# Layer 0's output weights applied to a pair of blocks by seven products of quarters

## The chip, the core and the metric

The kernel runs on one core of one Trainium2 chip. The metric is the device time of one execution in microseconds. TensorE (PE) does the matmuls, with its weight loads shown as PEld; VectorE (DVE) and ScalarE (ACT) work on tiles; GpSimd (POOL) and SyncE (SP) mostly issue DMAs.

## What is computed

Two layers over 2048 tokens of 1024 channels, each with a gated residual; the change lies in the first, a chunked gMLP:

```python
u, v, gate = jnp.split(h @ w_in, 3, axis=-1)          # h: normalised, modulated x
u = jax.nn.gelu(u)
v = _layernorm(jax.nn.gelu(v), vn_g, vn_b)
s = jnp.einsum('gpq,bnqgc->bnpgc', w_s, vc) + b_s...  # vc: v in chunks of 128 tokens
y = u * s.reshape(bn, L, A_WIDTH)                     # A_WIDTH = 2048
return (y * jax.nn.silu(gate)) @ w_out                # w_out: 2048 x 1024
...
x = x + gate[:, None] * y
```

Layer 1 is a multi-scale pooling mixer of the same widths, followed by a last RMSNorm. All of it is in float32.

## The kernel before

Channels lie on partitions, tokens along the free axis. The 2048 tokens are four blocks of 512 (`TB`), worked on in pairs of 1024 (`W2`). Every float32 product is made of three matmuls over operands that are split into a high and a low part (`mm3`, lines 103 to 107): high by high, low by high, high by low. `put` (lines 109 to 112) makes the split: ACT casts to the high part (L110), DVE subtracts to get the low part (L111).

Layer 0 runs for each pair of blocks:

- `v_phase`: the v branch, for the pair.
- `b_phase0`: for each c of 8, two channel chunks of u and of the gate. Each is a `unit` of seven products of quarters (Strassen's scheme in Winograd's form: seven products in place of eight, with sums of quarters of the rows and of the weights ahead of the products and sums of products after them). `mix(c)` does the spatial product and DVE multiplies. The result for each chunk and block, a tile `s`, goes to `y_d` in DRAM by a DMA that POOL issues (L930).
- `c_phase` (called from `c_phase0`) for each of the two blocks apart, the output stage: 16 channel chunks of y, by 8 output chunks d, by three matmuls of 512 columns into eight PSUM banks `po`. Four such calls make the layer's output, 4 x 16 x 8 x 3 = 1536 matmuls. At the end of a call each bank is scaled by the gate and added to x, by DVE (L945) or by ACT and DVE in turn, and stored in `x1_d`.

Operands come through a `Stream`: an ordered list of jobs, each a load that SP issues and a split. `get(i)` sees to it that jobs up to i + `ahead` are split, and loads run up to `LEAD` jobs further. Loads land in `raw` tiles (6 in layer 0); y comes into tiles `s`. Split pairs have 9 places.

Work that nothing near needs is put in a queue, `side`, and `do_side(n)` runs n of its steps at fixed points: one after each product of a unit. In `b_phase0` of the first pair it holds the RMS statistics of the next two blocks (`fetched_rms`, squares summed in a tile `ra`, each over a freshly loaded tile `x`) and five groups of `ada_late` steps (a step loads an `x` tile of 512 columns and DVE multiplies and adds it into `ra`, L444; after eight of them TensorE sums over partitions, `pm`, L450). In the output stage it holds `sum_steps`, which makes the row quarters of the next pair: 60 DVE instructions in all. In the second `v_phase` it holds `sum_quarters`, which makes sums of quarters of a weight ahead of their use and keeps them in DRAM.

TensorE works in the order in which the instructions stand in its queue, as each engine does; a layer of the language below the kernel sets that order from the order of the code and the dependences.

Of the kernel before, what the change touches and what calls it, by code (L numbers as in the profile page):

```python
# [12 lines left out]
F32 = mybir.dt.float32  # L13
F32R = mybir.dt.float32r
AF = mybir.ActivationFunctionType
ALU = mybir.AluOpType

P = 128
D = 1024
L = 2048  # L20
# [43 lines left out]
def hybrid_kernel(ctx: ExitStack, tc: tile.TileContext, a: dict):  # L64
# [11 lines left out]
    x1_d = dram.tile([KD, P, L], F32, name="x1_d")  # L76
    x2_d = dram.tile([KD, P, W2], F32, name="x2_d")
    v_d = dram.tile([2, 8, P, 8, 2 * P], F32, name="v_d")
    y_d = dram.tile([NC, P, L], F32, name="y_d")
    y1_d = dram.tile([NC, P, L], F32, name="y1_d")  # L80
    bt_d = dram.tile([8, P, 2 * P], F32, name="bt_d")

# [8 lines left out]
    def work(tag, width=512):  # L91
        return wk.tile([P, WK[tag][0]], F32, name=tag, tag=tag, bufs=WK[tag][1])[:, 0:width]
# [22 lines left out]
    def do_side(n=1000):  # L115
        for _ in range(min(n, len(side))):
            side.popleft()()
# [4 lines left out]
    def st_load(dst, src):  # L122
        st.last = nc.sync.dma_start(dst, src).ins

    def load(dst, src):

        with tc.issue_after(st.last):
            nc.sync.dma_start(dst, src)
# [10 lines left out]
    def split(src):  # L139
        p = new_pair()  # L140
        put(p, src)
        return p
# [147 lines left out]
        return [two_units(unit_jobs(lambda kh, c=c: a["g_wu"][c, kh]), unit_jobs(lambda kh, c=c: a["g_wg"][c, kh]), False)  # L290
                for c in range(8)]

    def y0_job(c, b):
        box = []

        def load():
            box.append(work("s"))
            st_load(box[0], y_d[c, :, b * TB:(b + 1) * TB])

        return load, lambda: split(box[0])  # L300

    def c_jobs(y, w):

        jobs = []
        for c in range(0, NC, 2):
            h = [half_jobs(lambda c=c: w[c]) for c in (c, c + 1)]
            i = st.add(y(c), h[0][0], y(c + 1), h[1][0], h[0][1], h[1][1])
            jobs.append(((i[0], i[2]), (i[1], i[3]), (i[4], i[5])))
        return jobs

    def c0_jobs(b):
        return c_jobs(lambda c: y0_job(c, b), a["g_wo"])

    def y1_job(c, t0, n, pair):
        box = []
# [40 lines left out]
    for b in (0, 2):  # L356
        jv.append(v_jobs())
        jug.append(ug_jobs())
        jc0 += [c0_jobs(b), c0_jobs(b + 1)]

    def pg_jobs():
        return [two_units(unit_jobs_made(c, partial(wf, c)),
# [95 lines left out]
    def ada_late(i, *gs):  # L458
        return [f for g in gs for f in ada_steps(i, g, 4, lambda: work("x"), lambda: work("ra"))]
# [258 lines left out]
    def rhs_lhs(g):  # L718
        return jf[g]

    def sum_quarters(c, q):

        box = []

        def fetch():
            for kh in range(2):
                for o in (0, 512):
                    box.append(work(("x", "x", "ra", "th")[len(box)]))
                    nc.gpsimd.dma_start(box[-1], q(kh)[:, o:o + 512])

        def sums():
            b11, b12, b21, b22 = box
            tc.keep_in_program_order(nc.vector.tensor_sub(b11, b12, b11))
            nc.vector.tensor_sub(b12, b22, b12)
            nc.vector.tensor_sub(b22, b22, b11)
            nc.vector.tensor_sub(b21, b21, b22)
            for j in range(4):
                nc.gpsimd.dma_start(t_d[c, j // 2, :, (j % 2) * 512:(j % 2) * 512 + 512], box[j])

        return [fetch, sums]  # L740

# [124 lines left out]
    def spatial(pb, stats):  # L866
# [39 lines left out]

        return fetch, normalise, mix

    def b_phase0(bb, rows, stats):
        st.ahead = 4  # L910
        fetch, normalise, mix = spatial(bb, stats)
        fetch(0)
        normalise(0)
        for c in range(8):
            gu = [work("g") for _ in range(4)]
            u = unit(rows, jug[bb][c][0], gu, lambda j: nc.scalar.activation(gu[j], gu[j], AF.Gelu_apprx_tanh))
            for i, pn in enumerate(ORDER):
                u(pn)
                if i == 3:
                    ss = mix(c)  # L920
            for j in (0, 2, 3, 1):
                nc.vector.tensor_mul(ss[j], ss[j], gu[j])
            gt = [work("g") for _ in range(4)]

            def gate(j):
                cc, t0 = 2 * c + j % 2, bb * W2 + (j // 2) * TB
                s = ss[j]
                nc.scalar.activation(gt[j], gt[j], AF.Silu)
                nc.vector.tensor_mul(s, s, gt[j])
                nc.gpsimd.dma_start(y_d[cc, :, t0:t0 + TB], s)  # L930

            g = unit(rows, jug[bb][c][1], gt, gate)
            for i, pn in enumerate(ORDER):
                g(pn)
                if c < 7 and i == 0:
                    fetch(c + 1)
                if c < 7 and i == 3:
                    normalise(c + 1)
        do_side()

    def residual(d, x, po, gate, turns=True):
# [35 lines left out]
            residual(d, x, po[d][:, 0:n], gate)  # L977
            nc.gpsimd.dma_start(store[d, :, t0:t0 + n], x)

    def c_phase0(b):  # L980
        c_phase(jc0[b], b * TB, TB, a["xT"], mod[0], "s", x1_d)


    tsum = [sum_quarters(c, partial(wf, c)) for c in range(8)]


    side.extend(late[1] + bias_steps())
# [3 lines left out]
    for b in (2, 3):  # L991
        rms, steps = fetched_rms(src0(b), TB, "ra", "x", 5)
        rms0.append(rms)
        side.extend(steps)
    side.extend(ada_late(0, 16, 20) + ada_late(1, 0, 4, 8))
    b_phase0(0, rows, stats)
    rows = Rows(0, [src0(2), src0(3)], rms0)
    sums = rows.sum_steps(lambda: work("g"))
    side.extend(sums[:9])
    c_phase0(0)  # L1000
    side.extend(sums[9:])
    c_phase0(1)
    do_side()


# [9 lines left out]
    b_phase0(1, rows, stats)  # L1015
    rows = Rows(1, [src1(0), src1(1)], rms1)
    sums = rows.sum_steps(lambda: work("g"))
    side.extend(sums[:9])
    c_phase0(2)
    side.extend(sums[9:])  # L1020
    c_phase0(3)
    do_side()
    l0_stack.close()
    st.end = len(st.jobs)
# [229 lines left out]
```

## Time and profile before

| | us |
|---|---|
| median of 3 runs (lowest to highest) | 2464.91 (2464.88 to 2468.14) |
| the profiled execution | 2464.14 |
| its span | 2462.4 |
| PE busy | 2429.4 (99%) |
| DVE busy | 1844.7 (75%) |
| ACT busy | 1086.6 (44%) |
| mean moved by DMA | 170 GB/s (169 GB/s of HBM reads and writes) |

Shares are of the span. A matmul's entry lasts longer than the time until the next one starts, since they are pipelined; the time that one costs is the distance between starts. The same holds, to a smaller degree, for DVE instructions in a row.

### The profile page before, as it was taken

The numbers are of one execution on the slowest core, as the hardware profiler recorded it, in microseconds if no ns is written. First come the engines' busy times: TensorE is split into PE (matmuls) and PEld (weight loads), VectorE is DVE, ScalarE is ACT, GpSimd is POOL, SyncE is SP. The second block draws the span as 40 slices with busy tenths as digits, with TensorE's granted clock in tenths as the row PEclk, the third lists the DMA queues.
The fourth block names the chain that finished last, engine by engine and source line by source line (L and its number), as shares of the span: only waits on it lengthen the run. The fifth ranks groups of instructions, "written<-read, shape, count | busy, mean of one in ns | idle before, by whom it ended". The sixth has DMA issues, their size and how long they took to land.

```text
span 2462.4 us, 32915 instructions
## 1 busy us (share of the span) xinstructions
PE 2429.4 (99%) x11392; PEld 2045.7 (83%) x11392; DVE 1844.7 (75%) x3079; ACT 1086.6 (44%) x1862; POOL 259.3 (11%) x478
## 2 busy tenths in 40 slices
PE   8999999999999999999999999999999999999998
PEld 7768888888878888888888888888878888888998
DVE  6785788887854678877878548788876498988656
ACT  5844544443643445444436433333354333333533
POOL 2211100000000332000000001011000001100011
PEclk9999999999999999999999999999999999999999
DMA  9733434554664666343536644432457545445764
GB/s 351 266 122 112 149 123 135 157 170 133 220 219 163 226 222 209 115 135 111 172 121 219 234 146 149 141 106 99 141 184 238 179 139 178 139 144 166 226 194 145
DMA packets 170966, 418.43 MB, mean 170 GB/s; under 512 B 21408, under 2 KB 45984, under 8 KB 169776
## 3 DMA queue, kind: packets, MB, share of 16 engines
q1 hardware_dynamic: 138960, 314.01, 40.2%
q0 software_dynamic: 27808, 97.57, 10.8%
q10 hardware_dynamic: 4032, 4.75, 0.7%
q8 instruction: 90, 1.47, 0.2%
q14 instruction: 76, 0.62, 0.1%
HBM read 327.16 MB, written 89.10 MB: 169 GB/s over the span
## 4 chain that ended last, share of the span: by engine, by line
PE 76%; issue 14%; DVE 4%; DMA 4%; POOL 1%; ACT 1%; SPq 0%; POOLq 0%; DVEq 0%; ACTq 0%
PE pu L104 13%; PE pu L106 13%; PE pu L105 13%; PE po L106 8%; PE po L104 8%; PE po L105 8%; PE pa L104 2%; PE pa L105 2%; PE pa L106 2%; PE psp L896 2%; PE pv L105 1%; PE pv L104 1%; PE pv L106 1%; DMA raw<-in_pool_wpT 1%; DVE wlo L111 1%
## 5 line engine op out<-in xcount | busy, mean ns | idle before, releaser
L110 ACT CAST whi<-raw 128x512 fp32r<-128x512 f32 x816 | 492.3, 618 | 674.7 <-PE pu L105 265.8
L111 DVE TENSOR_TENSOR wlo<-raw,whi 128x512 fp32r<-128x512 f32 x816 | 548.5, 685 | 257.8 <-ACT whi L110 254.2
L104 PE MATMUL pu<-S,whi 128*128 128x512 f32 x1024 | 400.9, 392 | 0.0
L106 PE MATMUL pu<-S,wlo 128*128 128x512 f32 x1024 | 398.7, 389 | 0.0
L105 PE MATMUL pu<-S,whi 128*128 128x512 f32 x1024 | 398.5, 389 | 0.0
L104 PE MATMUL po<-whi 128*128 128x512 f32 (+1 forms) x768 | 299.9, 390 | 4.4 <-ACT whi L110 4.4
L106 PE MATMUL po<-whi,wlo 128*128 128x512 f32 (+1 forms) x768 | 299.8, 391 | 1.0 <-DVE wlo L111 1.0
L104 PE MATMUL pu<-A,whi 128*128 128x512 f32 x768 | 300.0, 391 | 0.0
L105 PE MATMUL po<-wlo,whi 128*128 128x512 f32 (+1 forms) x768 | 299.1, 390 | 0.0
L106 PE MATMUL pu<-A,wlo 128*128 128x512 f32 x768 | 299.0, 389 | 0.0
L105 PE MATMUL pu<-A,whi 128*128 128x512 f32 x768 | 298.8, 389 | 0.0
L106 PEld LDWEIGHTS pu<-S,wlo 128*128 128x128 f32 x1024 | 192.2, 188 | 40.4
L104 PEld LDWEIGHTS pu<-S,whi 128*128 128x128 f32 x1024 | 192.3, 188 | 39.2
L105 PEld LDWEIGHTS pu<-S,whi 128*128 128x128 f32 x1024 | 192.3, 188 | 39.0
L104 PEld LDWEIGHTS po<-whi 128*128 128x128 f32 x768 | 144.5, 188 | 36.1 <-ACT whi L110 6.1
L106 PEld LDWEIGHTS po<-whi,wlo 128*128 128x128 f32 x768 | 144.5, 188 | 33.1 <-DVE wlo L111 2.8
L105 PEld LDWEIGHTS po<-wlo,whi 128*128 128x128 f32 x768 | 144.4, 188 | 30.1
L106 PEld LDWEIGHTS pu<-A,wlo 128*128 128x128 f32 x768 | 144.1, 188 | 30.3
L105 PEld LDWEIGHTS pu<-A,whi 128*128 128x128 f32 x768 | 144.2, 188 | 29.6
L104 PEld LDWEIGHTS pu<-A,whi 128*128 128x128 f32 x768 | 144.2, 188 | 29.6
L104 PE MATMUL po<-big,whi 128*128 128x388 f32 (+1 forms) x384 | 123.2, 321 | 0.0
L105 PE MATMUL po<-big,whi 128*128 128x388 f32 (+1 forms) x384 | 122.8, 320 | 0.0
(232 smaller groups left out, 3935.6 us busy)
## 6 DMA issues: line engine op xcount, KB each, us to landing
raw<-in_g_wo SPq DMA_DIRECT2D x64, 512.0 KB, 4.2
raw<-in_p_wo SPq DMA_DIRECT2D x96, 256.0 KB, 3.2
v_d<-g POOLq DMA_DIRECT2D x64, 256.0 KB, 3.1
raw<-in_g_wu SPq DMA_DIRECT2D x32, 512.0 KB, 4.1
raw<-in_g_wg SPq DMA_DIRECT2D x32, 512.0 KB, 4.9
raw<-v_d SPq DMA_DIRECT2D x32, 512.0 KB, 4.6
y_d<-s POOLq DMA_DIRECT2D x64, 256.0 KB, 2.9
x<-in_ada_w SPq DMA_DIRECT2D x64, 256.0 KB, 3.1
```

Source lines behind the costliest of these rows:

```text
L104: nc.tensor.matmul(out, w[0], x[0], start=first and not onto, stop=False, skip_group_check=onto)
L105: nc.tensor.matmul(out, w[0], x[1], start=False, stop=False, skip_group_check=onto)
L106: nc.tensor.matmul(out, w[1], x[0], start=False, stop=last, skip_group_check=onto)
L110: nc.scalar.copy(pair[0], src)
L111: nc.vector.tensor_sub(pair[1], src, pair[0].bitcast(F32))
L896: nc.tensor.matmul(p[:, t * P:(t + 1) * P], vt[h][:, t * 2 * P + j * P:t * 2 * P + (j + 1) * P], bw[:, 0:P], start=True, stop=True)
```

## The change

The output stage of layer 0 now takes both blocks of a pair together and is itself done by seven products of quarters. The quarters of the operand are, for each k of 8, the two channel chunks of that k by the two blocks; the quarters of the weights are two chunks of 128 rows by two halves of 512 output channels. One of the seven products is 8 values of k by 4 output chunks by 3 matmuls, so that a pair takes 7 x 96 = 672 matmuls and the layer 1344.

- **Row sums.** After each c of `b_phase0`, `row_sums` makes four sums of the four `s` tiles on DVE and stores them through POOL. Of the four `s` tiles three are stored as they are, so that `y_d` gets seven tiles for each c in place of four.
- **Weight sums.** `sum_quarters` makes four sums for each k once, in the `side` queue of the first `b_phase0` (8 times 4 DVE instructions, 4 loads and 4 stores through POOL, spaced out by empty steps), and keeps them in `to_d`. Both pairs read them.
- **Pace.** In the gate's unit two side steps run after each product in place of one.
- **Output stage.** `c_pairs` replaces `c_phase` for layer 0. Each step loads two tiles of 128x512 (one of y, one of weights) into one `raw` tile, splits both, and runs 12 matmuls. After each product four DVE instructions add the banks to x (`onto`): 28 for a pair, where 16 DVE and 8 ACT instructions stood. x is loaded through POOL four tiles at a time. `LEAD` is 8 there.
- `sum_steps` runs evenly over the 56 steps of the pair's output stage.

```diff
-    y_d = dram.tile([NC, P, L], F32, name="y_d")
+    y_d = dram.tile([2, 8, 7, P, TB], F32, name="y_d")
+    to_d = dram.tile([8, 2, P, W2], F32, name="to_d")
...
+    CORDER = (1, 2, 6, 5, 7, 3, 4)
+
+    def co_jobs(y, w, t):
+
+        src = {1: lambda k: w(k, 0)[:, 0:512], 2: lambda k: w(k, 1)[:, 0:512], 3: lambda k: w(k, 1)[:, 512:W2],
+               5: lambda k: t[k, 0][:, 0:512], 7: lambda k: t[k, 0][:, 512:W2],
+               4: lambda k: t[k, 1][:, 0:512], 6: lambda k: t[k, 1][:, 512:W2]}
+
+        def two(k, pn):
+            box = []
+
+            def load():
+                box.append(raw_tile())
+                st_load(box[0][:, 0:512], y(k, pn))
+                st_load(box[0][:, 512:W2], src[pn](k))
+
+            return (load, lambda: split(box[0][:, 0:512])), (None, lambda: split(box[0][:, 512:W2]))
+
+        return {pn: [st.add(*two(k, pn)) for k in range(8)] for pn in CORDER}
...
+    def row_sums(bb, k, y, t):
+
+        for pn, out, p, q, op in ((5, t[0], y[2], y[3], ALU.add), (6, t[1], t[0], y[0], ALU.subtract),
+                                  (7, y[2], y[0], y[2], ALU.subtract), (3, t[2], y[1], t[1], ALU.subtract)):
+            nc.vector.tensor_tensor(out, p, q, op)
+            nc.gpsimd.dma_start(y_d[bb, k, pn - 1], out)
+
...
             def gate(j):
-                cc, t0 = 2 * c + j % 2, bb * W2 + (j // 2) * TB
-                s = ss[j]
                 nc.scalar.activation(gt[j], gt[j], AF.Silu)
-                nc.vector.tensor_mul(s, s, gt[j])
-                nc.gpsimd.dma_start(y_d[cc, :, t0:t0 + TB], s)
+                nc.vector.tensor_mul(ss[j], ss[j], gt[j])
+                if j != 2:
+                    nc.gpsimd.dma_start(y_d[bb, c, (0, 1, None, 3)[j]], ss[j])
 
             g = unit(rows, jug[bb][c][1], gt, gate)
             for i, pn in enumerate(ORDER):
-                g(pn)
+                g(pn, 2)
...
+            side.appendleft(partial(row_sums, bb, c, ss, gt))
         do_side()
...
-    def c_phase0(b):
-        c_phase(jc0[b], b * TB, TB, a["xT"], mod[0], "s", x1_d)
+    def c_pairs(jobs, tokens, n, x_src, gate, tiles, store):
+
+        st.ahead, st.LEAD = 4, 8
+        total, steps = len(side), 0
+        xs, pa, pv = {}, [], []
+
+        def fetch(h, nh, tags):
+            for i in range(4):
+                x = work(tags[i], n)
+                nc.gpsimd.dma_start(x, x_src[nh * 4 + i, :, tokens[h]:tokens[h] + n])
+                xs[h, nh, i] = x
+
+        def onto(h, nh, banks, last):
+            for i in range(4):
+                d, x = nh * 4 + i, xs[h, nh, i]
+                nc.vector.scalar_tensor_tensor(x, banks[i][:, 0:n], gate[:, 16 + d:17 + d], x, ALU.mult, ALU.add)
+                if last:
+                    nc.gpsimd.dma_start(store[d, :, tokens[h]:tokens[h] + n], x)
+
+        use = {1: ((0, 0), 0), 2: ((0, 0), 1), 6: ((0, 1), 0), 5: ((1, 1), 0), 7: ((1, 1), 1), 3: ((0, 1), 1), 4: ((1, 0), 1)}
+        begin = {1: 0, 6: 0, 5: 1, 4: 1}
+        for pn in CORDER:
+            chain = pa if pn in (1, 6, 7, 4) else pv
+            if pn in (1, 2, 5):
+                chain[:] = [bank("po") for _ in range(4)]
+            for k in range(8):
+                y, w = (st.get(i) for i in jobs[pn][k])
+                for i in range(4):
+                    mm3(chain[i][:, 0:n], part(w, every, slice(i * P, (i + 1) * P)), part(y, every, slice(0, n)),
+                        k == 0, k == 7, pn in (6, 7, 4, 3))
+                if k == 3 and pn in begin:
+                    fetch(*use[pn][0], tiles[begin[pn]])
+                steps += 1
+                do_side(total * steps // 56 - (total - len(side)))
+            onto(*use[pn][0], chain, use[pn][1])
+        st.LEAD = 4
...
+    tsum_o = [sum_quarters(to_d[k], lambda h, k=k: a["g_wo"][2 * k + h]) for k in range(8)]
...
-    side.extend(ada_late(0, 16, 20) + ada_late(1, 0, 4, 8))
+    side.extend(spaced(tsum_o) + ada_late(0, 16, 20) + ada_late(1, 0, 4, 8))
...
-    side.extend(sums[:9])
+    side.extend(sums)
     c_phase0(0)
-    side.extend(sums[9:])
-    c_phase0(1)
```

The change also moves instructions. DVE's queue of the kernel before, in the first pair's unit stage, around the end of the sixth c (`ra` is the sum of an `ada_late` group, `g` and `s` the unit's results, `pu` its banks):

```order
L178 TENSOR_TENSOR raw_4914<-raw_4914 128x512
L180 TENSOR_TENSOR t2_5077<-raw_4915,raw_4914 128x512
L186 TENSOR_TENSOR raw_4914<-raw_4915,raw_4914 128x512
L181 TENSOR_TENSOR raw_4915<-raw_4915,t2_5077 128x512
L679 TENSOR_TENSOR g_4944<-g_4945,pu_4981 128x512
L111 TENSOR_TENSOR wlo_5081<-raw_4915,whi_5080 128x512
L111 TENSOR_TENSOR wlo_5110<-t2_5077,whi_5109 128x512
L452 TENSOR_TENSOR mod1_149<-pm_5016,smalls_121 128x4
L442 TENSOR_SCALAR ra_5074<-x_5040,cond_145 128x512
L929 TENSOR_TENSOR s_4841<-s_4841,g_4944 128x512
L444 SCALAR_TENSOR_TENSOR ra_5074<-x_5042,cond_145,ra_5074 128x512
L111 TENSOR_TENSOR wlo_5139<-raw_4914,whi_5138 128x512
```

In the change one `ada_late` group ends (L456, L464) and the next one begins (L454) at that place, and the four row sums (L925) stand between them, among the low parts (L112) of the next products; the change's line numbers are higher (L111 is L112, L442 L454, L444 L456, L452 L464, L929 L946):

```order
L456 SCALAR_TENSOR_TENSOR ra_4723<-x_4813,cond_146,ra_4723 128x512
L706 TENSOR_TENSOR g_4644<-g_4644,pu_4825 128x512
L464 TENSOR_TENSOR mod0_149<-pm_4842,smalls_122 128x4
L112 TENSOR_TENSOR wlo_4858<-raw_4616,whi_4857 128x512
L946 TENSOR_TENSOR s_4556<-s_4556,g_4644 128x512
L925 TENSOR_TENSOR g_4643<-s_4563,s_4570 128x512
L112 TENSOR_TENSOR wlo_4884<-raw_4616,whi_4883 128x512
L925 TENSOR_TENSOR g_4644<-g_4643,s_4549 128x512
L925 TENSOR_TENSOR s_4563<-s_4549,s_4563 128x512
L925 TENSOR_TENSOR g_4645<-s_4556,g_4644 128x512
L454 TENSOR_SCALAR ra_4902<-x_4848,cond_146 128x512
```

From mixing to mixing of the first pair stood 56 to 66 DVE instructions; in the change 65, 72, 57, 68, 68, 71 and 74, and 49 from the last mixing to the last `pm`. In the second pair it is 69, 60, 68, 65, 70, 61 and 56.

DVE's queue in the change, the end of the second product of the first output stage (A11, A12, A22 and S1 are row quarters of the next pair, L622 and L629 sums for them, L1014 the first of four `onto`):

```order
L112 TENSOR_TENSOR wlo_6072<-raw_5962,whi_6071 128x512
L112 TENSOR_TENSOR wlo_6091<-raw_5985,whi_6090 128x512
L112 TENSOR_TENSOR A22_5954<-g_5858,A22_5953 128x512
L622 TENSOR_TENSOR g_5858<-g_5856,g_5858 128x512
L112 TENSOR_TENSOR wlo_6095<-raw_5985,whi_6094 128x512
L112 TENSOR_TENSOR wlo_6122<-raw_6008,whi_6121 128x512
L112 TENSOR_TENSOR S1_5959<-g_5858,S1_5958 128x512
L629 TENSOR_TENSOR g_5856<-g_5852,g_5856 128x512
L112 TENSOR_TENSOR wlo_6126<-raw_6008,whi_6125 128x512
L1014 SCALAR_TENSOR_TENSOR s_5767<-po_5895,mod0_149,s_5767 128x512
```

Between the ends of two products stand 31, 31, 30, 23, 30, 16 and 23 other DVE instructions in the first pair's stage (the first count begins at the last row sums), 25, 31, 29, 22, 30, 16 and 16 in the second's.

SP's queue in the output stage before held loads of weights of 1024 columns and of y of 512 columns, and loads of x for the residual and the next pair:

```order
L128 DMA g_6312<-in_xT 128x512
L123 DMA raw_6332<-in_g_wo 128x1024
L123 DMA raw_6377<-in_g_wo 128x1024
L123 DMA s_6192<-y_d_77 128x512
L128 DMA s_6236<-in_xT 128x512
L128 DMA x_6146<-in_xT 128x512
L123 DMA raw_6430<-in_g_wo 128x1024
```

In the change it holds one load of y and one of weights or their sums for each step, and the x for the residual has moved to POOL's queue:

```order
L124 DMA raw_6308<-y_d_77 128x512
L124 DMA raw_6308<-to_d_78 128x512
L124 DMA raw_6348<-y_d_77 128x512
L124 DMA raw_6348<-to_d_78 128x512
L124 DMA raw_6371<-y_d_77 128x512
L124 DMA raw_6371<-to_d_78 128x512
```

## Rows read from the trace of the kernel before

**Rows 1.** The page's first part: span, then busy time by engine.
```profile
span 2462.4 us, 32915 instructions
...
PE 2429.4 (99%) x11392; PEld 2045.7 (83%) x11392; DVE 1844.7 (75%) x3079; ACT 1086.6 (44%) x1862; POOL 259.3 (11%) x478
```

**Rows 2.** TensorE's timeline at both output stages: start us, us, engine, line, instruction.
```profile
621.03 0.39 PE L104 MATMUL po<-whi 128*128 128x512 f32 x1
...
801.19 0.39 PE L104 MATMUL pa<-whi,A 128*128 128x512 f32 x1
...
1295.50 0.39 PE L104 MATMUL po<-whi 128*128 128x512 f32 x1
...
1469.96 0.39 PE L104 MATMUL po<-whi 128*128 128x512 f32 x1
...
1470.64 0.39 PE L104 MATMUL pu<-A,whi 128*128 128x512 f32 x1
```

**Rows 3.** TensorE's waits over the run: us in total, times, longest.
```profile
PE po L104 <- ACT whi L110: 4.4, 4, 1.9
...
PE pr L515 <- DVE ra L507: 2.7, 2, 2.2
...
PE pss L491 <- DVE ra L483: 1.6, 1, 1.6
```

**Rows 4.** Windows: PE, PEld, DVE, ACT, POOL busy (count), clock, DMA share, GB/s.
```profile
2.00:62.00 60.00, 55.32 (x238) 44.66 (x239) 41.04 (x58) 30.43 (x57) 16.12 (x21) 0.97 0.98 363
508.00:550.00 42.00, 42.00 (x206) 35.42 (x205) 39.27 (x67) 18.75 (x30) 2.16 (x4) 1.00 0.56 183
621.00:720.00 99.00, 97.79 (x430) 80.36 (x429) 73.10 (x119) 58.50 (x101) 5.41 (x10) 1.00 0.70 223
640.00:665.00 25.00, 25.00 (x112) 20.71 (x111) 25.00 (x43) 19.29 (x34) 0.00 (x0) 1.00 0.65 204
720.00:801.00 81.00, 78.61 (x341) 64.33 (x340) 37.40 (x59) 29.19 (x51) 2.16 (x4) 0.98 0.53 179
801.00:965.00 164.00, 163.78 (x724) 135.47 (x722) 120.63 (x207) 71.87 (x123) 61.69 (x100) 1.00 0.66 223
1290.00:1380.00 90.00, 89.47 (x394) 73.66 (x394) 70.05 (x114) 57.01 (x98) 2.70 (x5) 1.00 0.68 218
1380.00:1470.00 90.00, 90.00 (x398) 74.28 (x397) 43.68 (x69) 32.82 (x58) 5.41 (x10) 1.00 0.53 182
```

**Rows 5.** VectorE's timeline in two stretches without a wait.
```profile
543.94 0.74 DVE L444 SCALAR_TENSOR_TENSOR ra<-x,cond,ra 128x512 f32<-128x512 f32 x1
544.61 0.68 DVE L186 TENSOR_TENSOR raw<-raw 128x512 f32<-128x512 f32 x1
...
643.69 0.68 DVE L111 TENSOR_TENSOR S<-g,S 128x512 fp32r<-128x512 f32 x1
644.29 0.68 DVE L111 TENSOR_TENSOR wlo<-raw,whi 128x512 fp32r<-128x512 f32 x1
```

**Rows 6.** Groups by line: count | busy us, mean ns | idle before, releaser.
```profile
L111 DVE TENSOR_TENSOR wlo<-raw,whi 128x512 fp32r<-128x512 f32 x816 | 548.5, 685 | 257.8 <-ACT whi L110 254.2 <-PE po L105 1.0 <-PE pf L105 0.3
...
L444 DVE SCALAR_TENSOR_TENSOR ra<-x,cond,ra 128x512 f32<-128x512 f32 x56 | 41.8, 747 | 7.8 <-DMA x<-in_ada_w 7.5
```

**Rows 7.** The chain in order of time: two spatial mixings in a row.
```profile
375.38 3.57 PE psp L896 x32
...
418.01 3.57 PE psp L896 x32
```

**Rows 8.** DMA issues: queue, count, KB each, median us from issue to landing.
```profile
raw<-in_g_wo SPq DMA_DIRECT2D x64, 512.0 KB, 4.2
raw<-in_p_wo SPq DMA_DIRECT2D x96, 256.0 KB, 3.2
...
x<-in_ada_w SPq DMA_DIRECT2D x64, 256.0 KB, 3.1
...
g<-in_xT SPq DMA_DIRECT2D x24, 256.0 KB, 6.2
```

More of the change, by code (lines that the diff above doesn't have):

```diff
@@ L291, in ug_jobs @@
                 for c in range(8)]
[L293 to L300, printed above, removed]
+    CORDER = (1, 2, 6, 5, 7, 3, 4)
[11 more added lines that the diff above has]
+        return {pn: [st.add(*two(k, pn)) for k in range(8)] for pn in CORDER}
     def c_jobs(y, w):
@@ L309, in c_jobs, with c0_jobs @@
         return jobs
-    def c0_jobs(b):
-        return c_jobs(lambda c: y0_job(c, b), a["g_wo"])
+    def c0_jobs(pb):
+        return co_jobs(lambda k, pn: y_d[pb, k, pn - 1], lambda k, h: a["g_wo"][2 * k + h], to_d)
     def y1_job(c, t0, n, pair):
@@ L358, in hybrid_kernel @@
         jug.append(ug_jobs())
-        jc0 += [c0_jobs(b), c0_jobs(b + 1)]
+        jc0.append(c0_jobs(b // 2))
     def pg_jobs():
@@ L719, in rhs_lhs, with sum_quarters @@
         return jf[g]
-    def sum_quarters(c, q):
+    def sum_quarters(dst, q):
         box = []
@@ L737, in sums @@
             for j in range(4):
-                nc.gpsimd.dma_start(t_d[c, j // 2, :, (j % 2) * 512:(j % 2) * 512 + 512], box[j])
+                nc.gpsimd.dma_start(dst[j // 2, :, (j % 2) * 512:(j % 2) * 512 + 512], box[j])
         return [fetch, sums]
@@ L978, in c_phase, with c_phase0 @@
             nc.gpsimd.dma_start(store[d, :, t0:t0 + n], x)
-    def c_phase0(b):
-        c_phase(jc0[b], b * TB, TB, a["xT"], mod[0], "s", x1_d)
-    tsum = [sum_quarters(c, partial(wf, c)) for c in range(8)]
+    def c_pairs(jobs, tokens, n, x_src, gate, tiles, store):
[30 more added lines that the diff above has]
+        st.LEAD = 4
+    def c_phase0(pb):
+        c_pairs(jc0[pb], (pb * W2, pb * W2 + TB), TB, a["xT"], mod[0], (("s",) * 4, ("x", "x", "ra", "th")), x1_d)
+    tsum = [sum_quarters(t_d[c], partial(wf, c)) for c in range(8)]
+    tsum_o = [sum_quarters(to_d[k], lambda h, k=k: a["g_wo"][2 * k + h]) for k in range(8)]
     side.extend(late[1] + bias_steps())
@@ L1017, in hybrid_kernel @@
     sums = rows.sum_steps(lambda: work("g"))
[L1018 to L1021, printed above, removed]
+    side.extend(sums)
+    c_phase0(1)
     do_side()
```

## The prediction, made before the change was run

> **What bounds the kernel now.** I read the page's first part, then TensorE's waits, then the output stages in the timeline and stretch by stretch, then VectorE's and the DMAs' rows there. TensorE is busy for 2429.4 of 2462.4 us [rows 1]: whatever takes matmuls away is gained, unless something else then becomes late. Matmuls of 512 columns start 0.68 us apart by threes, so one costs 0.2267 us [rows 2]. TensorE's largest waits in the stages concerned are small: 4.4 us for the split of an operand of `po`, 2.7 and 1.6 us for VectorE's part of the RMS statistics [rows 3]. The next engine is VectorE: in the unit stage it is busy for 39.27 of 42 us, and in the output stage it once fills 25.00 of 25 us while TensorE fills them too [rows 4]. So a full VectorE does not stop TensorE as long as its queue puts the splits early; but there is little left to add.
>
> The sum is made against the profiled execution, 2464.1 us, which is 0.8 us below the median shown.
>
> **Matmuls removed.** 1536 become 1344; 192 x 0.2267 = **-43.5 us**, all on the path, since TensorE hardly waits there.
>
> **The seam between two blocks.** The first pair's output stage lasts from 621.03 to 801.19 us, 180.2, and the second's from 1295.50 to 1470.64, 175.1 [rows 2]. By price 768 matmuls are 174.1. The first thus loses 6.1 us, the second 1.0; the clock of 0.98 in 720:801 [rows 4] is part of the first. The loss lies where one block's residual holds the `s` tiles that the next block's y needs. With y in `raw` tiles and one stage for both blocks that seam is gone: 6.1 - 1.0 = **-5.1 us**. The 1.0 is kept, since the stage still starts on freshly stored y.
>
> **The unit stage of the first pair.** Each c gets four row sums and four weight sums on VectorE. Starts in a run are 0.60 us apart for a two-tile instruction and 0.67 for a multiply-add [rows 5], so 8 x 0.60 = 4.8 us for each c, beside TensorE's 42.63 us from mixing to mixing [rows 7]. The densest stretch shown has 67 instructions in 39.27 us, 0.586 each [rows 4]. By the queue, the last stretches of the change hold 71 and 74 between mixings and 49 up to the last `pm`: 194 x 0.586 = 113.7 us. TensorE's work there is 2 x 42.63 + 10 x 12 x 0.2267 = 112.5. VectorE is over by 1.2 us without any idle time; with that stretch's own idle time, 2.73 in 42, it is over by 8.5. The lead of four products does not hide this: each `pm` on TensorE waits for the eighth multiply-add of its group on VectorE, and behind it on TensorE stands the next product. I take **+6 us**, nearer the upper end, because 508:550 is the same work, and keep 1 to 9. Queued behind the new steps on POOL are the stores of y, 7 for each c in place of 4; their tiles `s` are wanted again only three to four products (8 to 11 us) after the row sums, against 3 us for a 256 KB transfer [rows 8].
>
> **The output stage.** A step has 12 matmuls, 2.72 us, and two splits; a product 8 steps, 21.8 us. VectorE has 112 low parts, 28 multiply-adds onto x and 60 instructions of `sum_steps` for a pair: 172 x 0.60 + 28 x 0.67 = 122 us of 152.3. It is not even: by the queue the first three and the fifth product hold 30 or 31 instructions beside four multiply-adds, 20.7 to 21.3 us, so 0.5 to 1.1 us are free in each. ScalarE has less (58.50 of 99 us before [rows 4]). After a product VectorE first waits for its end, then does 2.7 us of multiply-adds, while TensorE lives on two steps split ahead, 5.4 us. The lower bound is no wait, as in 640:665; the upper is one step lost in each of the five densest products of each pair, 27 us. I take **+4 us** for both pairs, near the lower end, which is a row of this very stage.
>
> **The loads.** Before, the first pair's stage moved 223 x 99 + 179 x 81 = 36.6 MB [rows 4]. Of these, y was 32 x 0.262 and weights 32 x 0.524 MB, 25.2; now they are 112 x 0.262 = 29.4. So 40.8 MB in 152.3 us, 268 GB/s. At 223 GB/s the engines' share was 0.70, which makes 319 GB/s at full share; 2:62 shows 363 [rows 4]. The stage would run at 0.84: covered, by six `raw` tiles or some 13 us of lead. Its cost is in the +4, and without that cover it is the last rival below.
>
> **The unit stage of the second pair** gets the row sums alone: 56 to 70 instructions between mixings, 41.0 us at most, under 42.63. The RMS and `pm` steps now come two to a product, so that their waits have half the distance. Nearest rows: 1.6 and 2.7 us for such waits [rows 3]. **+1.5 us**, from 0 to 5. `sum_steps` later in the stage, the sums in the second v stage and layer 1 change nothing: row quarters are ready some six steps before the end.
>
> Sum: 2464.1 - 43.5 - 5.1 + 6 + 4 + 1.5 = 2427.0; as a median, **2428 us**.
>
> **Rivals.**
>
> *Nothing new is late*: 2464.9 - 48.6 = 2416. For it: 640:665. Against it: the overload of the last stretches.
>
> *The steps of `ada_late` wait for their loads.* Two `x` tiles take turns, so a step cannot be faster than half of landing plus multiply-add: (3.1 + 0.67) / 2 = 1.9 us [rows 5, 8]. The gate's unit now wants two in 2.72 us, and 21 in 42.63 us on average, 2.03 each. At 3.1 us it just fits. Half way to the 6.2 us of the x loads for the next pair [rows 8] a step takes 2.7 us, and 40 of them are 25 us late: 2428 - 6 + 25 = 2447. For it: those loads already cost VectorE 7.5 us [rows 6], at half the pace.
>
> *VectorE's instructions cost their full length.* The low part's mean is 685 ns [rows 6], 1.14 times the 0.60 between starts. At 0.67 us for each instruction in the unit stages the counts that exceed 42.63 us do so by 30 us in the first pair and 12 in the second, and the dense products of the output stages by 14: 2416 + 56 = 2472. Against it: rows 5, and 67 instructions in 39.27 us. The Trainium skill, "VectorE: DVE Perf Modes", section "The DRAIN you can't avoid", says that the next instruction starts only once the pipe has emptied, and its section "The TRN2 errata" gives 691 ns for an fp32 two-tile instruction of 512 elements; by these, read together, this rival would be the forecast. The trace agrees with the length and not with the distance.
>
> *The transfers become the bound*, which is slower than before. If a mixed stage sustains no more than the 223 GB/s that two stretches reached [rows 4], the 40.8 MB take 183 us for each pair, 366 for both where 355.3 stood; with the unit stages' 7.5, 2464.9 + 10.7 + 7.5 = 2483. It decides below some 235 GB/s. For it: loads of 512 KB become two of 256 KB, 3.2 us each where one of 512 KB took 4.2 [rows 8]. Against it: a share of only 0.66 to 0.70 at 223, and 363 GB/s in 2:62. The Trainium skill, "DMA: Bandwidth & Descriptors", section "Bandwidth", asks for 1 MiB in a transfer and gives 341 GB/s there and 138 at 64 KB; this speaks against the change. By these rows transfers in flight together make up for their size.
>
> That the matmuls are not removed can be left out: the queue holds 672 `po` matmuls for a pair.
>
> **How the numbers follow.** Forecast with 3 to 25 us of new waits, 2419 to 2441: 0.70. Nothing late: 0.13. Late `ada_late` loads: 0.08. Full length: 0.03. Transfers: 0.06. The range of 2415 to 2446 leaves out the last three, 0.17. Two tenths of a per cent (4.9 us) is about what a measurement can tell from no change: faster 0.90 (the first three but for a tail of the third), within it 0.02 (that tail and one of the fourth), slower 0.08.
>
> **What would show it.** Right: 1344 `po` matmuls of 512 columns in layer 0, two output stages of 152 to 157 us, no gap in their middle, VectorE near 0.8 and DMA near 0.84 there, waits of TensorE for `ra` at `pm` late in the first unit stage, of a few us. Wrong: waits for whi or wlo in each product whose releaser is a load (transfers), VectorE idle before L456 (loads of `x`), or VectorE full with TensorE waiting in both unit stages (its price).

## The result and the profile after

The change takes 2439.86 us (median of 4 runs, 2437.09 to 2445.77) where the kernel before took 2466.52 on the same chip (4 runs, 2464.88 to 2469.89): ratio 0.9893, 95% interval 0.9869 to 0.9917. It is faster by about 1.1%. 2428 was forecast, from 2415 to 2446.

The first part of the profile page of the change answers to [rows 1]:

```profile
span 2435.3 us, 33160 instructions
PE 2391.0 (98%) x11200; PEld 2014.6 (83%) x11200; DVE 1932.7 (79%) x3231; ACT 1089.4 (45%) x1878; POOL 338.2 (14%) x622
```

The span fell by 27.1 us. To see where, I took the times at which TensorE's first matmul of each stage starts, as in [rows 2]. In the timeline of TensorE in the change these are the first output stage, the second v stage, the second output stage and layer 1:

```profile
642.46 0.77 PE L105 MATMUL po<-whi 128*128 128x512 f32 x1
...
797.47 0.39 PE L105 MATMUL pa<-whi,A 128*128 128x512 f32 x1
...
1291.84 0.39 PE L105 MATMUL po<-whi 128*128 128x512 f32 x1
...
1444.17 0.39 PE L105 MATMUL pu<-A,whi 128*128 128x512 f32 x1
```

| stretch | before, us | after, us | difference | forecast |
|---|---|---|---|---|
| start to the end of the first unit stage | 621.03 | 642.46 | +21.4 | +6 |
| first output stage | 180.16 | 155.01 | -25.2 | -24.8 |
| second v and unit stages | 494.31 | 494.37 | +0.1 | +1.5 |
| second output stage | 175.14 | 152.33 | -22.8 | -19.8 |
| layer 1 | 991.8 | 991.1 | -0.6 | 0 |

(The forecast splits the 4 us of new waits evenly between the output stages, and has the 1.0 us that was kept in both: 672 x 0.2267 + 1.0 + 2 = 155.3 each.) The output stages gave 48.0 us and the first unit stage took 21.4 back. TensorE's waits in that stretch, 285 to 660 us of the change:

```profile
PE pm L462 <- DVE ra L456: 12.9, 2, 10.5
PE pm L462 <- ACT g L945: 2.8, 1, 2.8
```

Before, it waited for no `pm` there; its only wait in 285 to 660 us of the kernel before was at the start of the output stage:

```profile
PE po L104 <- ACT whi L110: 1.0, 1, 1.0
```

Now it stops three times, 15.7 us in all, where it wants the sum over partitions of an `ada_late` group. The third stop is put down to ScalarE, but there too VectorE's last multiply-add of the group ends only at 640.82, 0.15 us before the `pm` starts. The rest of the 21.4 stands in the next view, the stretches of the change, whose column PEclk (after POOL's) is the granted clock:

```profile
457.00:500.00 43.00, 43.00 (x208) 36.19 (x207) 38.82 (x66) 18.10 (x30) 14.09 (x27) 1.00 0.76 248
500.00:543.00 43.00, 33.91 (x166) 28.36 (x164) 37.13 (x62) 15.69 (x27) 11.14 (x21) 0.95 0.71 234
543.00:588.00 45.00, 43.55 (x206) 36.94 (x207) 40.27 (x70) 16.57 (x28) 4.04 (x7) 0.93 0.62 201
...
642.00:795.00 153.00, 153.00 (x665) 126.58 (x666) 126.34 (x206) 87.72 (x153) 15.89 (x30) 0.98 0.81 271
1294.00:1450.00 156.00, 156.00 (x690) 129.16 (x689) 125.34 (x203) 87.89 (x154) 17.61 (x33) 1.00 0.77 254
```

In the longest stop, and just behind the two others, the granted clock falls, and it stays down for a few us of matmuls. The timeline of TensorE around the longest stop:

```profile
533.52 0.39 PE L107 MATMUL pu<-S,wlo 128*128 128x512 f32 x1
544.45 1.87 PE L462 MATMUL pm<-ones,ra 128*128 128x1 f32 x8 [10.54 <-DVE ra L456]
...
547.18 0.63 PE L107 MATMUL pu<-A,wlo 128*128 128x512 f32 x1
547.61 0.63 PE L105 MATMUL pu<-A,whi 128*128 128x512 f32 x1
...
549.43 0.40 PE L107 MATMUL pu<-A,wlo 128*128 128x512 f32 x1
549.66 0.40 PE L105 MATMUL pu<-A,whi 128*128 128x512 f32 x1
```

A matmul lasts 0.63 us in place of 0.39 there and starts come 0.43 apart in place of 0.23: the 1.2 GHz level. The granted clock of 538.8 to 549.0 us is 0.50. Slow matmuls behind the three stops, those of `pm` among them, make up some 5 of the other 5.7 us of the stage (21.4 - 15.7), and 2.7 us of the first output stage, which starts behind the third stop. VectorE's share of the longest stop is in its own timeline, the rows of `ada_late` alone:

```profile
526.34 0.49 DVE L454 TENSOR_SCALAR ra<-x,cond 128x512 f32<-128x512 f32 x1 [0.66 <-DVE wlo L112]
527.07 0.75 DVE L456 SCALAR_TENSOR_TENSOR ra<-x,cond,ra 128x512 f32<-128x512 f32 x1
532.10 0.75 DVE L456 SCALAR_TENSOR_TENSOR ra<-x,cond,ra 128x512 f32<-128x512 f32 x1 [1.51 <-DMA x<-in_ada_w]
...
543.65 0.75 DVE L456 SCALAR_TENSOR_TENSOR ra<-x,cond,ra 128x512 f32<-128x512 f32 x1
```

The first of the group's eight steps starts at 526.3 us and the last ends at 544.4; TensorE had come to the group's `pm` at 533.9. What made the group late was open: the views allow several causes.

### The profile page after: what moved, and what is told of

Its sections match the earlier page's. It is cut to its first block, busy times and chain, and to the rows that moved or that the text cites. A ratio compares the mean times of both kernels' runs of the same rounds, so it can differ in the third digit from the quotient of the medians.

```text
span 2435.3 us, 33160 instructions
## 1 busy us (share of the span) xinstructions
PE 2391.0 (98%) x11200; PEld 2014.6 (83%) x11200; DVE 1932.7 (79%) x3231; ACT 1089.4 (45%) x1878; POOL 338.2 (14%) x622
## 4 chain that ended last, share of the span: by engine, by line
PE 84%; DVE 6%; DMA 6%; issue 2%; ACT 1%; SPq 0%; POOL 0%; DVEq 0%; POOLq 0%; ACTq 0%
PE pu L105 15%; PE pu L107 15%; PE pu L106 15%; PE po L105 9%; PE po L107 9%; PE po L106 9%; PE pa L105 2%; PE pa L106 2%; PE pa L107 2%; PE psp L908 2%; PE pv L107 1%; PE pv L105 1%; PE pv L106 1%; DVE wlo L112 1%; DMA x<-in_ada_w 1%
## 5 line engine op out<-in xcount | busy, mean ns | idle before, releaser
L111 ACT CAST whi<-raw 128x512 fp32r<-128x512 f32 x912 | 539.0, 617 | 614.7 <-PE pu L106 224.5
L112 DVE TENSOR_TENSOR wlo<-raw,whi 128x512 fp32r<-128x512 f32 x912 | 606.0, 686 | 172.4 <-ACT whi L111 167.2
L105 PE MATMUL po<-whi 128*128 128x512 f32 (+1 forms) x704 | 275.4, 391 | 0.5 <-ACT whi L111 0.5
L107 PE MATMUL po<-whi,wlo 128*128 128x512 f32 (+1 forms) x704 | 275.2, 391 | 0.3 <-DVE wlo L112 0.3
L106 PE MATMUL po<-wlo,whi 128*128 128x512 f32 (+1 forms) x704 | 275.0, 391 | 0.0
L107 PEld LDWEIGHTS po<-whi,wlo 128*128 128x128 f32 x704 | 132.7, 189 | 29.0 <-DVE wlo L112 1.0
L105 PEld LDWEIGHTS po<-whi 128*128 128x128 f32 x704 | 132.9, 189 | 28.4 <-ACT whi L111 0.9
L106 PEld LDWEIGHTS po<-wlo,whi 128*128 128x128 f32 x704 | 132.9, 189 | 27.9
```

What stands on the lines that cost most here:

```text
L105: nc.tensor.matmul(out, w[0], x[0], start=first and not onto, stop=False, skip_group_check=onto)
L106: nc.tensor.matmul(out, w[0], x[1], start=False, stop=False, skip_group_check=onto)
L107: nc.tensor.matmul(out, w[1], x[0], start=False, stop=last, skip_group_check=onto)
L111: nc.scalar.copy(pair[0], src)
L112: nc.vector.tensor_sub(pair[1], src, pair[0].bitcast(F32))
```

## Experiments

Three theories stood at the start, to which the expectations refer. **A**: VectorE has too many instructions in the last stretches of the first unit stage. **B**: the `ada_late` steps, two to a product in the gate's unit, wait for their own loads, which go into two tiles `x` in turn. **C**: the eight rounds of weight sums (four loads, four sums, four stores, all through POOL and over the same four tiles) are slow, and stand in VectorE's queue ahead of the `ada_late` groups. **D** came up after eleven runs: the distance in TensorE's queue between a group's steps and its `pm`. The last two columns, and every view below, come from one traced execution of each kernel.

| run | time, us | ratio to before, interval | `pm` waits, first unit stage | first output starts |
|---|---|---|---|---|
| the change | 2439.86 | 0.9893, 0.9869 to 0.9917 | 15.7 | 642.5 |
| e1 | 2437.04 | 0.9898, 0.9883 to 0.9912 | 2.1 | 621.3 |
| e2 | 2434.22 | 0.9890, 0.9876 to 0.9905 | 11.7 | 636.2 |
| e3 | 2451.33 | 0.9965, 0.9951 to 0.9980 | 17.3 | 645.2 |
| e4b | 2429.35 | 0.9859, 0.9842 to 0.9875 | 9.7 | 635.5 |
| e5 | 2426.68 | 0.9855, 0.9839 to 0.9871 | 3.3 | 628.5 |
| e6 | 2435.92 | 0.9886, 0.9870 to 0.9902 | 7.8 | 634.1 |
| e7 | 2420.63 | 0.9826, 0.9809 to 0.9842 | none | 618.6 |
| e9 | 2431.82 | 0.9867, 0.9847 to 0.9887 | 5.2 | 628.2 |
| e10 | 2424.27 | 0.9837, 0.9821 to 0.9854 | none | 622.7 |
| e11 | 2424.90 | 0.9834, 0.9815 to 0.9852 | none | 621.6 |
| e12 | 2429.08 | 0.9855, 0.9841 to 0.9870 | 3.9 | 631.3 |

### The order of the rounds and the groups

**e1** puts the groups first.

```diff
-    side.extend(spaced(tsum_o) + ada_late(0, 16, 20) + ada_late(1, 0, 4, 8))
+    side.extend(ada_late(0, 16, 20) + ada_late(1, 0, 4, 8) + spaced(tsum_o))
```

> The same work; in the first unit stage the five ada_late groups stand ahead of the weight sums in the side queue, not behind them. Three theories of the 15.6 us in which TensorE waits at pm there (10.5, 2.3 and 2.8 us). (A) VectorE has too many instructions: its load is the same, so the waits at pm stay at 8 us or more, the time within 5 us of the change (2435 to 2445 us). (B) The ada_late steps wait for their own loads, two tiles x in turn at two steps to a product: they still come two to a product, so the waits stay at 8 us or more, as under A, but VectorE's idle time before L456 grows or stays (6 us or more). (C) The groups start late because the round of load, sum and store of the weight sums, over the same tiles x and ra, stands before them in VectorE's queue: nothing on TensorE waits for the sums soon, so the waits at pm fall below 4 us in all and the time to about 2420 to 2427 us.

The waits for `pm` all but vanish, as C said, but the time hardly falls. TensorE's waits in 285 to 790 us of e1 show why:

```profile
PE po L106 <- DVE wlo L112: 8.3, 2, 6.1
PE po L107 <- DVE wlo L112: 2.1, 2, 1.4
PE pm L462 <- DVE ra L456: 2.1, 1, 2.1
```

The rounds are still running when the output stage starts, and its low parts stand behind them. Some 13 of the 21 us moved: that stage takes 168.2 us where the change has 155.0. Besides, the groups' `pm` stand six and seven products behind their loads here (counted in `side`), where the change has five and nine, so that this run does not tell C from D.

**e2** takes three groups out of the stage.

```diff
-    side.extend(spaced(tsum_o) + ada_late(0, 16, 20) + ada_late(1, 0, 4, 8))
+    side.extend(spaced(tsum_o) + ada_late(0, 16, 20))
...
-    side.extend(ada_late(1, 12, 16, 20))
+    side.extend(ada_late(1, 0, 4, 8, 12, 16, 20))
```

> The same work; three of the five ada_late groups of the first unit stage are made in the second one instead, the weight sums stay first. A: VectorE's load in the last stretches of the first unit stage falls by some 17 us over the stage, so the waits at pm fall below 4 us there; 2422 to 2428 us. B: two groups are left in place of five, waits of about 40 per cent, 6 us; 2430 us. C: the first group still starts behind the weight sums; its wait of 10 us stays (8 us or more), that of the others goes; 2430 to 2435 us.

One stop of 11.7 us is left, at the first group behind the rounds, though 24 multiply-adds are gone from the stage. That is as C had it. It weighs little against A, since the multiply-adds taken out stand behind that group in the queue. (Its second unit stage, with six groups, is 6.9 us longer than the change's.)

### Taking work away

**e3** leaves the four row sums out (their stores stay), **e5** the weight sums (the products read plain quarters).

```diff
-            nc.vector.tensor_tensor(out, p, q, op)
```

> Leaves out the four row sums of each c on VectorE; their stores stay. A: 2.4 us less for each c of both unit stages, 10 us less ahead of and between the pm of the first one; waits at pm below 5 us, about 2425 us. B and C: the loads and the weight sums are as before, so the waits at pm stay at 9 us or more; 2432 to 2440 us.

```diff
-               5: lambda k: t[k, 0][:, 0:512], 7: lambda k: t[k, 0][:, 512:W2],
-               4: lambda k: t[k, 1][:, 0:512], 6: lambda k: t[k, 1][:, 512:W2]}
+               5: lambda k: w(k, 0)[:, 0:512], 7: lambda k: w(k, 0)[:, 512:W2],
+               4: lambda k: w(k, 1)[:, 0:512], 6: lambda k: w(k, 1)[:, 512:W2]}
...
-    side.extend(spaced(tsum_o) + ada_late(0, 16, 20) + ada_late(1, 0, 4, 8))
+    side.extend(ada_late(0, 16, 20) + ada_late(1, 0, 4, 8))
```

> Leaves out the weight sums (loads, VectorE instructions and stores); the output stage reads plain quarters of the weights in their place, as many bytes. The side queue of the first unit stage is shorter by 56 steps, so the ada_late groups come earlier and the stage's last third has none. A: 2.4 us less for each c, waits at pm below 6 us. B: the groups still come two steps to a product in the gate's unit; waits at pm of 6 us or more, VectorE idle before L456 of 6 us or more. C: waits at pm below 3 us; 2418 to 2424 us, which would be all the matmuls removed give.

e3 is slower than the change, which no theory had. VectorE has less to do and waits more for transfers; its waits in 285 to 650 us of e3 (5.5 and 7.4 us in the change for the first two):

```profile
DVE x L745 <- DMA x<-in_g_wo: 12.1, 4, 5.4
DVE raw L899 <- DMA raw<-v_d: 11.9, 9, 2.8
DVE ra L456 <- DMA x<-in_ada_w: 8.7, 10, 1.8
```

So fewer instructions on VectorE did not shorten the stops. This alone does not refute A, as the run also changes when loads come; why they come later stays open. e5 brings the output stage forward to 628.5: without any round 7.5 us of the 21.4 remain, with stops at `pm` again (3.3 us). So C is not the whole cause either. Here too the groups stand six and seven products ahead, so that what is gained is not the rounds' alone.

### Other places and tiles

**e4b** gives the `ada_late` loads a third tile and starts them two steps ahead.

```diff
-    def ada_steps(i, g0, ng, raw, acc_tile):
+    def ada_steps(i, g0, ng, raw, acc_tile, places=1):
...
-        row = ahead(KD, fetch, 1)
+        row = ahead(KD, fetch, places)
...
-        return [f for g in gs for f in ada_steps(i, g, 4, lambda: work("x"), lambda: work("ra"))]
+        turn = deque(("x", "x", "th"))
+
+        def raw():
+            turn.rotate(-1)
+            return work(turn[-1])
+
+        return [f for g in gs for f in ada_steps(i, g, 4, raw, lambda: work("ra"), 2)]
```

> The change, with a third tile (th) for the loads of the ada_late steps, two loads ahead in place of one. (B) If the steps wait for their own loads, half or more of the 15.6 us at pm goes and VectorE's idle time before L456 falls from 6 to below 2 us; ratio 0.985 to 0.987. (C) The first group is late because of what stands before it: the first wait at pm stays at 8 us or more; ratio 0.988 to 0.990.

2429.35 us, with an interval that just overlaps the change's. The stops fall from 15.7 to 9.7 us at the same distances, and the output stage starts 7.0 us earlier: the loads into two tiles have a part in it. But TensorE still stops for 7.0 us at the first group.

**e6** makes six of the eight rounds in the first v stage.

```diff
-    side.extend(late[1] + bias_steps())
+    side.extend(late[1] + bias_steps() + spaced(tsum_o[:6]))
...
-    side.extend(spaced(tsum_o) + ada_late(0, 16, 20) + ada_late(1, 0, 4, 8))
+    side.extend(spaced(tsum_o[6:]) + ada_late(0, 16, 20) + ada_late(1, 0, 4, 8))
```

> Six of the eight weight sums are made in the first v stage, where each has seven places of 2.7 us for its round of loads, sums and stores; two stay in the first unit stage ahead of the ada_late groups; the rest of the change as it is. (C) The round of the weight sums through POOL's queue and four tiles, some 12 us and more each at places that leave it 9.5 us in the gate's unit, makes the unit stage late: with six of them elsewhere the waits at pm fall below 4 us and the ratio to the kernel before to that without weight sums, 0.983 to 0.987. (A) VectorE's load: only the stretches with sums get lighter, the ada_late stretches at the end stay at 71 to 74 instructions, so the waits at pm stay at 6 us or more and the ratio at 0.987 to 0.990.

The stops halve, the first from 10.5 to 5.4 us, with each group's `pm` as many products behind its load as in the change. So the rounds have a part in it. The time is within the change's interval: C's figures are missed, and A's (6 us or more, 0.987 to 0.990) are met.

**e12** is e6 with e4b's three tiles.

> The change with six rounds of weight sums in the first v stage (e6) and a third tile for the ada_late loads (e4b), pace and groups as in the change. If loads into two tiles and rounds of weight sums add up (B and C), the waits for ra at pm in the first unit stage fall under 4 us, the output stage starts at 622 to 628 us and the time is 2418 to 2425 us, ratio 0.982 to 0.985. If the number of VectorE's instructions in the last stretches is the bound (A), nothing is gained over the better of the two: 2428 to 2436 us, ratio 0.985 to 0.989, with VectorE at 0.9 or more in the 86 us before its last pm and no wait for a load of over 0.5 us there.

The waits fall to 3.9 us, as B and C had it, the time is no better than e4b's, as A had it: no verdict. VectorE is busy for 80.9 of the 86 us from 457 to 543, but waits for loads up to 1.6 us, so that A's own condition is not met.

### Pace

**e7** is e6 with e2's groups in the second unit stage and one side step per product in the first.

```diff
-                g(pn, 2)
+                g(pn, 1 + bb)
```

> As the one with six sums in the v stage; besides, three ada_late groups go to the second unit stage, and the gate's unit of the first pair runs one side step to a product again (the second pair's keeps two). If the rest of the loss is the crowding of ada_late steps two to a product, TensorE's waits in both unit stages fall below 3 us and the ratio to 0.980 to 0.983, some 2413 to 2420 us: the matmuls removed and the seam, with nothing given back. If the row sums themselves are the price, 7 us stay and the ratio is 0.983 to 0.986.

2420.63 us, no stop at `pm`, and the output stage starts 24 us before the change's. **e9** takes the pace alone back.

> e7 with one part taken back: the gate's unit of the first pair runs two side steps per product again. Six rounds of weight sums stay in the first v stage and three ada_late groups in the second unit stage. If the rounds of weight sums alone hold VectorE's queue up (C), the first output stage starts at 617 to 622 us as in e7 and the time is 2418 to 2423 us, ratio 0.982 to 0.984. If two ada_late steps in one product are too many for loads into two tiles (B), TensorE waits 3 to 10 us again for ra at pm, the output stage starts at 624 to 634 us and the time is 2425 to 2435 us, ratio 0.985 to 0.989.

A stop of 5.2 us returns, as B had it, and 11.2 us of time (the intervals do not meet): what matters is how densely the side steps are queued. The pace is that of all steps in the gate's unit; e10 below narrows it to the groups'. e2 and e9 differ in the number of rounds ahead of the first group alone as far as this stage goes, eight and two: 11.7 and 5.2 us.

**e11** adds the third tile to e7.

> e7 with the third tile for the ada_late loads. The six groups in its second unit stage lengthen that stage by 9.6 us (504.0 from the end of the first output stage to the second's start, 494.4 in the change). If that is the loads into two tiles (B), the stage falls to 494 to 498 us and the time to 2409 to 2416 us, ratio 0.978 to 0.981. If it is VectorE's 24 more multiply-adds (A), it stays at 500 to 505 us and the time at 2416 to 2422 us, ratio 0.981 to 0.984.

e11 is not better than e7. The second unit stage stays long, 504.2 us, with stops at `pm` again (3.4 us), so B is not what lengthens it. The time is above what A gave, too.

**e10** tests the distance by itself: e2, and an empty step behind each step of the two groups.

```diff
-    side.extend(spaced(tsum_o) + ada_late(0, 16, 20))
+    side.extend(spaced(tsum_o) + [g for f in ada_late(0, 16, 20) for g in (f, rest)])
```

> e2 with an empty step after each step of the two ada_late groups in the first unit stage, so that a group's eight multiply-adds stand some ten products of the unit ahead of its pm on TensorE where they stood five. All eight rounds of weight sums still stand before them, and their number of VectorE instructions is the same. If the distance between a group's steps and its pm decides (a fourth theory, D), the wait for ra at pm falls from e2's 11.7 us to under 3 us, the first output stage starts at 619 to 626 us (e2 636.2) and the time is 2418 to 2427 us, ratio 0.982 to 0.986. If the rounds alone hold VectorE's queue up (C), the first wait stays at 8 us or more, the output stage starts at 632 us or later and the time is 2430 to 2438 us, ratio 0.987 to 0.990.

It came out as D had it: no stop, start at 622.7, 2424.27 us. The first group in e10, in VectorE's timeline and then TensorE's:

```profile
527.47 0.49 DVE L454 TENSOR_SCALAR ra<-x,cond 128x512 f32<-128x512 f32 x1 [0.44 <-DVE wlo L112]
528.19 0.75 DVE L456 SCALAR_TENSOR_TENSOR ra<-x,cond,ra 128x512 f32<-128x512 f32 x1
534.11 0.75 DVE L456 SCALAR_TENSOR_TENSOR ra<-x,cond,ra 128x512 f32<-128x512 f32 x1 [2.40 <-DMA x<-in_ada_w]
...
553.04 0.75 DVE L456 SCALAR_TENSOR_TENSOR ra<-x,cond,ra 128x512 f32<-128x512 f32 x1
```

```profile
562.79 0.95 PE L462 MATMUL pm<-ones,ra 128*128 128x1 f32 x8
```

The group starts on VectorE as late as in the change (527.5 and 526.3), waits for a load as well (2.40 us), and takes longer. But TensorE comes to its `pm` 29 us later, at 562.8 in place of 533.9, and nothing waits. By the places in `side` the `pm` stands thirteen products behind the group's load there, not the ten expected, since some of the twenty places fall into the next u's unit at one to a product. The empty steps give the loads more time as well, but the group took 26.3 us from its first step to its last, where the change took 18.1: faster loads are not what removed the stop. In the first and third of e10's stretches VectorE is fuller than in any of those of the change, beside a TensorE without a pause at full clock:

```profile
457.00:500.00 43.00, 43.00 (x207) 36.23 (x206) 41.91 (x71) 19.02 (x32) 16.16 (x30) 1.00 0.79 258
500.00:543.00 43.00, 43.00 (x207) 36.20 (x207) 36.28 (x62) 15.77 (x27) 11.26 (x21) 1.00 0.70 242
543.00:588.00 45.00, 45.00 (x221) 37.95 (x220) 44.82 (x77) 20.96 (x36) 5.35 (x10) 1.00 0.63 203
```

The change itself shows the same. Its five groups' `pm` stand five, nine, five, nine and five products behind their loads; the second and fourth reach into the next u's unit. The three stops are those at five. At the two others TensorE does not wait, though VectorE takes longer over them (24.7 and 23.4 us, against 18.1, 14.8 and 16.3), because TensorE comes to their `pm` 25.1 us after their first step on VectorE, and to the three after 7.6, 12.7 and 13.6. The `pm` of the second and third group in TensorE's timeline:

```profile
575.75 0.95 PE L462 MATMUL pm<-ones,ra 128*128 128x1 f32 x8
...
592.76 1.25 PE L462 MATMUL pm<-ones,ra 128*128 128x1 f32 x8 [2.31 <-DVE ra L456]
```

In the first unit stage of every run, each stop at `pm` is at a group of five or six products, and none of seven or more waits for over 0.1 us.

### The seam

**e8** is the kernel before with its residual tiles in `g` in place of `s`.

```diff
-        c_phase(jc0[b], b * TB, TB, a["xT"], mod[0], "s", x1_d)
+        c_phase(jc0[b], b * TB, TB, a["xT"], mod[0], "g", x1_d)
```

> The kernel before, with one thing changed: in layer 0's output stage half of the x tiles for the residual lie in tiles g, not s, so that the next block's y does not wait for them. If the seam is that wait, the first output stage falls from 180.2 to 175 or 176 us and the time by 3 to 5 us (ratio 0.998). If the seam is another wait (the banks, or y stored late), nothing changes (ratio 1.000).

2460.51 us, ratio 0.9988 (0.9978 to 0.9998): a gain of 0.5 to 5.4 us. Its first output stage, in TensorE's timeline, takes 175.2 us where [rows 2] have 180.2:

```profile
620.17 0.39 PE L104 MATMUL po<-whi 128*128 128x512 f32 x1
...
795.38 0.39 PE L104 MATMUL pa<-whi,A 128*128 128x512 f32 x1
```

So the seam was the wait for `s` tiles, and cost 5.0 us in this stage; 2.0 of them come back in the second v and unit stages of the traced execution (496.3 us, before 494.3), which stays open.

## Why the prediction held, and where it failed

The time lies in the range, but that is in part luck: the first unit stage lost 21.4 us where its own term allowed 1 to 9, and the output stages and the second unit stage came out 4.8 us better than forecast.

**Matmuls and seam** held. The second output stage takes 152.33 us, which is 672 times 0.2267, with no wait of TensorE at all; the first 155.01, of which 2.7 are the lower clock it starts with. The 5.1 us of the seam are confirmed by e8, and the 1.0 that was kept went too.

**The output stage's +4** was too much: no step is lost. VectorE is busy for 126.34 of 153 us and 125.34 of 156, near the 122 counted, and TensorE waits in neither stage, as in the row of 640:665 us, which was the lower bound.

**The loads** came as worked out: 271 and 254 GB/s at shares of 0.81 and 0.77 (268 at 0.84 forecast). The issues of the change, with KB and median us to landing:

```profile
raw<-y_d SPq DMA_DIRECT2D x112, 256.0 KB, 3.6
raw<-to_d SPq DMA_DIRECT2D x64, 256.0 KB, 4.1
raw<-in_g_wo SPq DMA_DIRECT2D x48, 256.0 KB, 3.8
```

Each is slower than the 3.2 us of [rows 8], yet TensorE waits for none. Nothing here bears out the rule of the Trainium skill ("DMA: Bandwidth & Descriptors", "Bandwidth") as a price for this stage.

**The first unit stage's +6** is the term that failed: +21.4. The step was to divide VectorE's instructions by TensorE's time and to charge the overload. It put the waits at the right place, at `pm` behind VectorE's eighth multiply-add, but by a sum that does not set them. e10 has the same instructions in this stage as e2, the row sums and all eight rounds among them, and loses nothing to `pm` in it where e2 stops for 11.7 us; e3 has 32 instructions fewer than the change and loses more. What sets them is the distance. A group is ten side steps; where all of them stand two to a product its `pm` stands five products, 13.6 us, behind its load, where one to a product gives some 27. Before, VectorE took 14 to 20 us for a group and TensorE came to the `pm` 27 to 31 us after its first step. The prediction named this halving, but only for the second pair, where it cost nothing: the three groups there stand six and seven products ahead. In the first pair VectorE needs 18 us for the first group, starts it late because the rounds hold its queue up (e6 beside the change, e2 beside e9), and waits for loads in it (e4b). Taking either away shortens the stop; the distance of thirteen products removes it with both still there. And the stop has a second price, which the term left out: the lower clock behind it, some 5 us in the stage and 2.7 after.

**Rivals.** *Loads of ada_late* was half there: e4b shows its part, and its sign, VectorE idle before L456, was there (6.1 us in 285 to 650 us, 3.7 before); but its 25 us assumed landing times half way to 6.2 us, where these loads land in 3.0 us, about as before. *Full length* is refuted: 77 VectorE instructions in 44.82 us in e10 are 0.58 us each, at a mean length of 0.67. The Trainium skill, "VectorE: DVE Perf Modes" ("The DRAIN you can't avoid"), read by itself as a distance between starts, is not what these rows show. *Transfers as the bound* is refuted by the output stages. *Nothing new is late* at 2416 is what e7 comes within 5 us of.

**A faster version.** e7 beats the change (the intervals do not meet); the intervals of e10 and e11 overlap with e7's. What e7 still pays is in the second unit stage, 504.0 us (771.41 to 1275.40 in TensorE's timeline) where the change has 494.4: six groups at two steps per product stop TensorE again, 2.9 us, and the granted clock is 0.96 from 1148 to 1232 us, where the stops lie. That the same cure works there was not tried; that stage's queue has no places left for so many empty steps.

## What to carry to other kernels

When side work is queued at a denser pace, count how far TensorE's instruction that needs its result stands behind its first step, and compare that with the time the other engine needs for the steps, its lateness included. In e10 an engine that is full delays nothing, as that distance is long; in the change one with room delays TensorE where it is short. How long is long enough depends on the stage: in e7's second unit stage the last three groups, six and seven products ahead, still stop TensorE for 0.3 to 1.5 us. Moving late work out of the way only pays if nothing near needs it where it goes (e1, and the second stage of e2 and e7).

## What the runs showed of the hardware

How many matmuls run at the lower level behind a stop does not follow from the length of the stop. The stops of 10.54 and 2.31 us in the change are each followed by seven matmuls of a product at the lower level; the third, of 2.78 us, by thirteen, the first ones of the output stage:

```profile
643.03 0.63 PE L106 MATMUL po<-wlo,whi 128*128 128x512 f32 x1
...
647.29 0.63 PE L107 MATMUL po<-whi,wlo 128*128 128x512 f32 x1
647.72 0.54 PE L105 MATMUL po<-whi 128*128 128x512 f32 x1
648.10 0.39 PE L106 MATMUL po<-wlo,whi 128*128 128x512 f32 x1
```

The granted clock there, in the column PEclk:

```profile
641.20:648.00 6.80, 6.80 (x21) 5.64 (x21) 3.99 (x8) 0.42 (x1) 4.77 (x9) 0.50 0.89 274
```

From 642.46 to 648.10 that is 5.6 us where thirteen matmuls take 2.95 at the higher level. With the slower `pm` (1.49 us to the next matmul, 0.81 at the higher level) the stop of 2.78 us cost some 6.2. So the price of a short stop can be about twice what the view of waits shows.
